# An encoder block's feed-forward: the change of halves, the border between its two products and its last steps rearranged

## The chip, the core and the metric

The kernel runs on one core of a Trainium2 chip. The metric is the device time of one execution in microseconds (us). The engines are PE (TensorE, matrix products), DVE (VectorE), ACT (ScalarE), POOL (GpSimd) and SP (SyncE, which here issues every transfer of this part from one queue). Each engine takes its instructions in a fixed order: one that waits holds up all that stand behind it on that engine, and the same holds for the transfers that SP issues.

## What is computed

One layer of a hybrid encoder (a recurrent and an attention group side by side, then a feed-forward), S = 2048 tokens, D = 1024 columns, 4096 hidden units. The change touches only the second sub-layer and the closing norm:

```
h2 = rms_norm(x, norm2_g) * (1 + scale2) + shift2
ff = square(relu(h2 @ w_ff1)) @ w_ff2
x = x + gate2 * ff
return rms_norm(x, final_g)
```

## The kernel before

The feed-forward (from some 1360 us to the end) is two matrix products in single precision. Each product takes seven products of block sums instead of eight products of blocks (Strassen's scheme); `LEFT` and `RIGHT` name for each of the seven, m = 1 to 7, the blocks whose sum or difference is its left and right operand. Every operand is split into a coarse half `hi` and a rest `lo` (`halves`: ACT rounds, DVE or POOL subtracts), and hi·hi, hi·lo and lo·hi are added up in PSUM. A sum or difference of blocks is made by `signed` (L1218), on the engine that its caller names.

**First product (FF1).** The tokens are two halves, a = 0 and 1. The hidden units are 16 block pairs p. `steps1` lists 224 steps (a, m, p), in the order of m 2, 4, 5, 3, 1, 6, 7 for one p after the other. A step is 12 matmuls of 128x512. `w1_prep` makes a step's left operand from two loaded blocks of W1, three steps ahead: `signed` on POOL where m takes two blocks, `hi` on ACT, `lo` on DVE (L1222, L1223), into one of six slots. The right operands (the normed tokens, `bks`) stand in SBUF for a whole half: `build2` writes those of m = 2, 4, 5, 3 by transposes, `b_prep` makes those of m = 1, 6, 7 in four chunks each: two loads from DRAM (`st<-Dh`, L1290, L1293), `signed` on POOL, `halves`. `sums2` makes the block sums of the second half ahead and stores them (`Dhc`); near the end of the first half `b_prep(1, m)` loads these and writes all seven operands anew. `evac1` adds the seven products to the four output blocks of p, applies relu and square, makes the sums which the second product needs as its right operands, and `put` (L1330) stores them to `Dhx[m][p]`.

**Second product (FF2).** `ORD2` = 4, 2, 7, 3, 5, 1, 6 is the order of m, `steps2` goes over 16 p for each m: 112 steps of 24 matmuls (8 token tiles by 3). `ld2` (L1488, L1491) loads two blocks of W2 and the hidden operand, three steps ahead; `prep2`, two steps ahead, makes the sum on DVE, `halves` it into `wf`, rounds the hidden operand on ACT (L1508) and takes its rest on POOL (L1510). At the last p of each m the tiles are finished one after the other, three matmuls apart, and `evac2` adds each to `C`, the output in SBUF. The gate is multiplied later: `resid` (L1545 times `gate2`, L1549 plus x1 loaded into `xt`), except that m = 6 gets it in `prep2` (L1500). `final` is the closing norm of a tile of 128 tokens by 1024: ACT squares and sums (L1555), the reciprocal root goes over DVE and one POOL instruction (`rstd_g`, L299 to L306), DVE scales (L1559), SP stores 512 KB (L1560). `finals` runs `resid` and `final` during m = 6; the second half of the tiles gets its `final` when its last product is done.

All first loads of FF2 stand in the program behind the last `put` of FF1. A list scheduler decides the order of the instructions of an engine near that of the program; the rows under "The change" show it.

Of the kernel before, what the change touches and what calls it, by code (L numbers as in the profile page):

```python
# [17 lines left out]
P = 128  # L18
S = 2048
# [37 lines left out]
def block_kernel(ctx: ExitStack, tc, x, vecs, pos, w_ada, b_ada, fg, w_in, lwa, lwx, w_out, w1, w2, cst, out):  # L57
# [412 lines left out]
    xrn = [sbt("L8", (P, S + 8)) for j in range(4)]  # L470
# [792 lines left out]

    def w1_prep(s):
# [14 lines left out]
    def b_prep(a, m):  # L1279
# [5 lines left out]
        def load(k):  # L1285
            t = [sbt("st", (P, 512))]
            if a and sg:
                SY.dma_start(t[0], Dhc[m][:, k])
            else:
                SY.dma_start(t[0], Dh2[a][x_ // 10, x_ % 10][:, k])  # L1290
                if sg:
                    t.append(sbt("st", (P, 512)))
                    SY.dma_start(t[1], Dh2[a][y_ // 10, y_ % 10][:, k])  # L1293
            q.append(t)
# [117 lines left out]

    PB = ("mm", "g", "tr", "mm", "g", "tr", "mm", "g")
# [4 lines left out]
    xslot += [t[:, 512 * e:512 * (e + 1)] for t in (sbt("bc", (P, D)), sbt("bc", (P, D))) for e in range(2)]  # L1418
# [4 lines left out]
    loads = [(p, u) for p in list(range(2, NP)) + list(range(NP)) for u in (1, 0)]  # L1423
# [3 lines left out]
    for s, (a, m, p) in enumerate(steps1):  # L1427
        if s == 6:
# [12 lines left out]
        w, (hi, lo) = wslot[(s + 4) % 6], bks[m]  # L1441
# [30 lines left out]
    BUFS.update({"C": NT, "xr": 4, "w2": 4, "wf": 4, "xt": 2, "row": 2})  # L1472
    sb[0] = ctx.enter_context(tc.tile_pool(name="f2", bufs=1, reuse_waits="tile"))
    ORD2 = (4, 2, 7, 3, 5, 1, 6)
    steps2 = [(m, p) for m in ORD2 for p in range(NP)]
    N2 = len(steps2)
    C = {}
    gate2, fgb = sbt("row", (P, D)), sbt("row", (P, D))
    raws2, wts2, hraw, hids = {}, {}, {}, {}
    TILES = {i: [8 + 4 * (i - 1) + e for e in range(4)] + [4 * (i - 1) + e for e in range(4)] for i in (1, 2)}  # L1480

    def ld2(s):
        m, p = steps2[s]
        x_, sg, y_ = RIGHT[m]
        t = sbt("w2", (P, 2, 512))
        for i, blk in enumerate((x_, y_) if sg else (x_,)):
            r0, j = (p + NP * (blk // 10 - 1)) * P, blk % 10 - 1
            SY.dma_start(t[:, i], w2[r0:r0 + P, 512 * j:512 * (j + 1)])  # L1488
        raws2[s] = (t[:, 0], t[:, 1])
        hraw[s] = sbt("xr", (P, 2, 512))  # L1490
        SY.dma_start(hraw[s], Dhx[m][p])  # L1491

    def prep2(s):
        m, p = steps2[s]
        x_, y_ = raws2.pop(s)
        if RIGHT[m][1]:
            t = sbt("st", (P, 512))
            signed(V, t, x_, RIGHT[m][1], y_)
            if m == 6:
                V.tensor_tensor(t, t, gate2[:, 512:], ALU.mult)  # L1500
        else:
            t = x_
        w = sbt("wf", (P, 2, 512), F32R)
        halves(t, w[:, 0], w[:, 1], V)
        wts2[s] = w
        r_ = hraw.pop(s)
        h = sbt("L8", (P, 2, 2, 512), F32R)
        A.activation(h[:, 0], r_, AF.Copy)  # L1508
        for e in range(2):
            G.tensor_tensor(h[:, 1, e], r_[:, e], f(h[:, 0, e]), ALU.subtract)  # L1510
        hids[s] = h.rearrange("p s a t -> p s (a t)")
# [136 lines left out]
```

## Time and profile before

| | |
|---|---|
| three runs | 2720.13, 2720.20, 2723.26 us; median 2720.2 us |
| the profiled execution | 2720.57 us, of which the span of the trace is 2718.7 us |
| busy share of the span | PE 94 %, DVE 61 %, ACT 40 %, POOL 44 % |
| mean granted clock of PE | 0.949 |
| HBM read and written | 330 MB and 153 MB, 178 GB/s over the span |

PE is busy nearly all the time. In the profile's forty slices the PE digit falls to 7 or 8 near 1400 us and at some later places, and to 6 in the last slice. The average shares of the other engines say little here: each of these stretches has a bound of its own, which the rows further down show.

### The profile page before, as it was taken

How to read it: one execution, taken by the hardware profiler on the slowest of the kernel's cores; microseconds unless marked ns; L12 is line 12 of the kernel's file. 1: busy time of each engine (PE TensorE's matmuls, PEld its weight loads, DVE VectorE, ACT ScalarE, POOL GpSimd, SP SyncE). 2: the span in 40 equal slices, each digit the busy share in tenths (PEclk: the TensorE clock that was granted, in tenths of full speed). 3: DMA queues.
4: the chain of work that ended last, by engine and by line, in shares of the span. 5: the costliest groups of instructions: out<-in, count | busy, mean ns of one | idle time of the engine just before them, and what ended most of it. 6: DMA issues, size and time to landing. Idle time of an engine off the chain costs nothing.

```text
span 2718.7 us, 32852 instructions
## 1 busy us (share of the span) xinstructions
PE 2542.2 (94%) x11321; PEld 2075.0 (76%) x11321; DVE 1656.9 (61%) x2963; ACT 1093.5 (40%) x1701; POOL 1200.8 (44%) x914
## 2 busy tenths in 40 slices
PE   4998988999999999999879999899998999999996
PEld 3776767778888888887757877688886888888885
DVE  6588777974444444436767657977774224312688
ACT  2243675571122222222455445655553323232223
POOL 2343444642012211131357667766556445544544
PEclk9998989998898888899989999999998999999998
DMA  6765356566544455547766666644437465536554
GB/s 266 266 225 186 96 178 211 203 163 159 122 109 118 117 132 140 125 141 235 243 202 214 204 195 209 209 152 155 140 129 276 164 209 187 170 121 210 191 201 176
DMA packets 267491, 486.01 MB, mean 179 GB/s; under 512 B 88874, under 2 KB 122406, under 8 KB 259754
## 3 DMA queue, kind: packets, MB, share of 16 engines
q1 hardware_dynamic: 267324, 483.92, 55.4%
q8 instruction: 89, 1.46, 0.2%
q14 instruction: 78, 0.64, 0.1%
HBM read 330.45 MB, written 153.19 MB: 178 GB/s over the span
## 4 chain that ended last, share of the span: by engine, by line
PE 36%; POOL 6%; DVE 5%; DMA 5%; issue 3%; ACT 1%; SPq 0%; POOLq 0%; DVEq 0%; ACTq 0%
PE pmm L89 15%; PE pg L89 13%; PE ptr L89 8%; POOL st L1218 3%; DMA st<-Dh 3%; POOL ry L301 1%; DVE L L1223 1%; POOL t L1380 1%; DMA Dhc<-st 1%; POOL L L1510 0%; DVE C L1545 0%; DVE C L1549 0%; DVE L L1200 0%; POOL L L1381 0%; DMA r<-in_w 0%
## 5 line engine op out<-in xcount | busy, mean ns | idle before, releaser
L1510 POOL TENSOR_TENSOR L<-xr,L 128x512 fp32r<-128x512 f32 x224 | 317.5, 1438 | 285.9 <-ACT L L1508 278.7
L89 PE MATMUL pmm<-hT,wh 128*128 128x512 f32 x1536 | 376.1, 401 | 5.9 <-POOL hT L341 3.3
L89 PEld LDWEIGHTS pmm<-hT,wh 128*128 128x128 f32 x1536 | 293.6, 193 | 78.3 <-POOL hT L341 7.7
L89 PE MATMUL pmm<-wf,L 128*128 128x512 f32 x1008 | 292.4, 398 | 17.8 <-ACT L L1508 12.8
L89 PE MATMUL pg<-wf,L 128*128 128x512 f32 x1008 | 290.0, 396 | 0.0
L858 DVE CUSTOM_DVE_ANT_0 junk<-ptr,mb 128x256 bf16<-128x256 f32 (+2 forms) x384 | 140.1, 365 | 174.3 <-PE ptr L89 157.3
L89 PEld LDWEIGHTS pmm<-wf,L 128*128 128x128 f32 x1008 | 190.5, 189 | 65.2 <-ACT L L1508 13.2
L912 ACT ACTIVATE t<-pmm 128x512 f32<-128x512 f32 x160 | 94.8, 596 | 353.5 <-PE pmm L89 352.3
L1223 DVE TENSOR_TENSOR L<-st,L 128x512 fp32r<-128x512 f32 x167 | 191.4, 1151 | 63.3 <-ACT L L1222 62.0
L89 PEld LDWEIGHTS pg<-wf,L 128*128 128x128 f32 x1008 | 190.7, 189 | 45.2
L257 POOL TENSOR_TENSOR wh<-r,wh 128x512 fp32r<-128x512 f32 x88 | 139.8, 1610 | 173.5 <-DVE wh L95 106.1
L301 POOL TENSOR_TENSOR ry<-rv,mhalf 128x1 f32<-128x1 f32 x80 | 51.5, 645 | 350.4 <-DVE rv L299 341.3
L89 PE MATMUL ptr<-wf,L 128*128 128x512 f32 x672 | 193.9, 397 | 0.0
L1218 POOL TENSOR_TENSOR st<-r,r 128x512 f32<-128x512 f32 x96 | 135.9, 1423 | 109.3 <-DVE L L1223 94.7
L89 PE MATMUL pmm<-hT,hT 66*128 66x256 f32 (+5 forms) x672 | 177.1, 399 | 0.0
L1223 DVE TENSOR_TENSOR wf<-st,wf 128x512 fp32r<-128x512 f32 x80 | 59.8, 747 | 190.6 <-ACT wf L1222 190.6
L1222 ACT ACTIVATE L<-st 128x512 fp32r<-128x512 f32 x168 | 105.5, 628 | 163.6 <-POOL st L1218 84.9
L89 PE MATMUL ptr<-hT,hT 128*128 128x256 f32 (+5 forms) x672 | 163.6, 390 | 4.1 <-DVE mc L858 4.0
L1222 ACT ACTIVATE wf<-st 128x512 fp32r<-128x512 f32 x80 | 50.4, 631 | 281.7 <-PE pg L89 216.5
L89 PE MATMUL pg<-t,L 128*66 128x192 f32 (+2 forms) x756 | 159.0, 348 | 1.8 <-POOL L L1051 1.8
L89 PE MATMUL pmm<-hT,L 128*128 128x512 f32 x576 | 149.7, 408 | 10.0 <-ACT L L1222 7.1
L89 PEld LDWEIGHTS pmm<-hT,hT 128*128 128x128 f32 (+1 forms) x672 | 148.8, 278 | 9.1 <-issue 2.6
(326 smaller groups left out, 5276.3 us busy)
## 6 DMA issues: line engine op xcount, KB each, us to landing
xr<-Dhx SPq DMA_DIRECT2D x112, 512.0 KB
w<-in_w SPq DMA_DIRECT2D x192, 256.0 KB
r<-in_w SPq DMA_DIRECT2D x64, 512.0 KB
Dhx<-t SPq DMA_DIRECT2D x128, 256.0 KB
L<-in_w_ada SPq DMA_DIRECT2D x24, 1024.0 KB
r<-in_w_in SPq DMA_DIRECT2D x40, 512.0 KB
st<-Dh SPq DMA_DIRECT2D x72, 256.0 KB
r<-in_x SPq DMA_DIRECT2D x26, 512.0 KB
```

What stands on the lines that cost most here:

```text
L89: T.matmul(o, l, r, start=st, stop=sp, skip_group_check=True)
L257: G.tensor_tensor(w[:, 1, cs], raw[:, cs], f(w[:, 0, cs]), ALU.subtract)
L301: G.tensor_tensor(y, v_, mhalf[:, 0:1], ALU.pow)
L858: V.tensor_tensor_reduce(junk[:, 0:nk], p_[:, e, 0:nk], mb1[:, off:off + nk], 1.0, -3e38, ALU.add, ALU.max, mc[:, idx:idx + 1])
L912: A.activation(pf, pS, AF.Exp)
L1218: eng.tensor_tensor(o, a, b, ALU.add if sign > 0 else ALU.subtract)
L1222: A.activation(hi, raw, AF.Copy)
L1223: lo_eng.tensor_tensor(lo, raw, f(hi), ALU.subtract)
L1380: G.tensor_tensor(x6, x6, h, ALU.subtract)
L1510: G.tensor_tensor(h[:, 1, e], r_[:, e], f(h[:, 0, e]), ALU.subtract)
```

## The change

1. Half change: the second half takes the block pairs in the order 15, 0, 1, ..., 14. The seven W1 operands of p = 15 stay in their slots from the end of the first half (there are seven slots then, the seventh in a `bc` buffer) and are neither loaded nor made again. `w_slot` deals the slots out in turn.
2. `signed` of W1 goes to DVE for all of the first twelve steps, and after that for m = 1, 5 and 6; m = 2 and 7 stay on POOL.
3. `b_prep(0, m)` loads its chunks into the four halves of two `bc` buffers (`braw`) instead of into `st` buffers.
4. The first two steps of FF2 are loaded (into `r4` buffers) and made ready (weights in W1 slots, hidden operands in `hT` buffers, half a gate row in `st`) during the last steps of FF1, and multiplied straight behind its last step. The other loads of FF2 stand behind that, and the full gate row (L1581 of the changed kernel) ahead of them.
5. The gate goes into W2 in `prep2` (one multiplication per step, 128x1024 for m = 1, 6 and 7, 128x512 for the rest). `C` is preset with x1 by 16 transfers of 512 KB, two in each of eight steps, so `evac2` only adds or subtracts, all on DVE. `resid` and its loads go.
6. `ff2_mm`: the last two p of each m (the last four for m = 6) are multiplied tile by tile, so a tile's sum is complete every 6 matmuls (every 12 for m = 6) instead of every 3.
7. The last norm: the tiles of TILES[1] get `final` during m = 6. For TILES[2], `halfway` takes the squares of the first 512 columns and multiplies them by the norm's weights during m = 1; `final2` does what is left after a tile's last product. Stores of TILES[2] are 256 KB.
8. `xrn`, a buffer of an earlier stage, is 56 columns wider.

The core of the diff:

```diff
-    xrn = [sbt("L8", (P, S + 8)) for j in range(4)]
+    xrn = [sbt("L8", (P, S + 64))[:, 0:S + 8] for j in range(4)]
...
-    steps1 += [(a, m, p) for a in range(2) for p in range(0 if a else 2, NP) for m in OA + OB]
+    steps1 += [(0, m, p) for p in range(2, NP) for m in OA + OB]
+    steps1 += [(1, m, p) for p in [NP - 1] + list(range(NP - 1)) for m in OA + OB]
...
     def w1_prep(s):
-        _, m, p = steps1[s]
+        a, m, p = steps1[s]
+        if a and p == NP - 1:
+            wuse[s] = wts1[m]
+            return
...
-            signed(G, t, x_, sg, y_)
-        w = wslot[(s + 4) % 6]
+            signed(V if s < 12 or m in (1, 5, 6) else G, t, x_, sg, y_)
+        w = wuse[s] = wts1[m] = w_slot()
...
         def load(k):
-            t = [sbt("st", (P, 512))]
-            if a and sg:
-                SY.dma_start(t[0], Dhc[m][:, k])
+            if a:
+                t = [sbt("st", (P, 512))]
+                SY.dma_start(t[0], Dhc[m][:, k] if sg else Dh2[a][x_ // 10, x_ % 10][:, k])
             else:
+                t = [braw[2 * (k % 2) + e] for e in range(2)]
                 SY.dma_start(t[0], Dh2[a][x_ // 10, x_ % 10][:, k])
...
+        t = sbt("w2" if s > 1 else "r4", (P, 2, 512))
...
+        hraw[s] = sbt("xr" if s > 1 else "r4", (P, 2, 512))
...
+        if sg and x_ % 10 != y_ % 10:
+            V.tensor_tensor(raw.rearrange("p a c -> p (a c)"), raw.rearrange("p a c -> p (a c)"), gate2[0],
+                            ALU.mult)
+        if sg:
+            t = sbt("st", (P, 512))
+            signed(V, t, raw[:, 0], sg, raw[:, 1])
+        if not sg or x_ % 10 == y_ % 10:
+            V.tensor_tensor(t, t, g_, ALU.mult)
+        w = sbt("wf", (P, 2, 512), F32R) if s > 1 else w_slot()
...
+        if s == N1 - 3:
+            gate2.append(sbt("st", (P, 512)))
+            SY.dma_start(gate2[0], Dbc[1][:, 0:512])
+            ld2(0)
+            ld2(1)
...
+        if s >= N1 - 2:
+            prep2(s - N1 + 2)
...
+    def ff2_mm(s, group, evac=None):
...
+        pend.append(s)
+        if NP - group <= p < NP - 1:
+            return
+        for i in range(8):
+            ts = slice(i * P, (i + 1) * P)
+            for q in pend:
...
+    for s in range(2):
+        ff2_mm(s, 2)
     stage.close()
...
+            signed(V, C[t][:, d], C[t][:, d], sg, pt)
+        if m == 6:
+            side.append(final2(i))
+            step(3)
+
+    fgb, gate2[0] = sbt("row", (P, D)), sbt("row", (P, D))
+    SY.dma_start(gate2[0], Dbc[1])
...
+    def halfway(i):
+
+        xt = C[TILES[2][i]][:, 0:512]
+        A.activation(junk[:, 0:512], xt, AF.Square, accum_out=ssa[:, i:i + 1])
+        yield
+        G.tensor_tensor(xt, xt, fgb[:, 0:512], ALU.mult)
+
+    def final2(i):
...
+        A.activation(junk[:, 512:], xt[:, 512:], AF.Square, accum_out=ss)
+        yield
+        V.tensor_tensor(ss, ss, ssa[:, i:i + 1], ALU.add)
+        for r in rstd_g(ss, D):
+            yield
+        A.activation(xt[:, 0:512], xt[:, 0:512], AF.Copy, scale=r[:, 0:1])
+        SY.dma_start(out[t * P:(t + 1) * P, 0:512], xt[:, 0:512])
+        V.scalar_tensor_tensor(xt[:, 512:], xt[:, 512:], r[:, 0:1], fgb[:, 512:], ALU.mult, ALU.mult)
+        SY.dma_start(out[t * P:(t + 1) * P, 512:], xt[:, 512:])
...
+        if s > 2:
+            for t in x1q[:2]:
+                SY.dma_start(C[t], Dx1[t])
+            del x1q[:2]
```

**Order on POOL, at the start of FF1.** Before, while the second half's last transposes are built (`r_...` are blocks of W1, `st<-st` are the chunks of `b_prep`):

```order
314 L1218 TENSOR_TENSOR st_10723<-st_10723,st_10725 128x512
315 L1218 TENSOR_TENSOR st_10751<-st_10751,st_10753 128x512
316 L1218 TENSOR_TENSOR st_10769<-r_1636_10660 128x512
317 L1218 TENSOR_TENSOR st_10755<-st_10755,st_10757 128x512
318 L1218 TENSOR_TENSOR st_10818<-r_1621_10595,r_1609_10514 128x512
319 L1218 TENSOR_TENSOR st_10762<-st_10762,st_10764 128x512
320 L1218 TENSOR_TENSOR st_10791<-st_10791,st_10793 128x512
321 L1218 TENSOR_TENSOR st_10908<-r_1609_10514,r_1621_10595 128x512
322 L1218 TENSOR_TENSOR st_10928<-st_10928,st_10930 128x512
323 L1218 TENSOR_TENSOR st_10946<-r_1621_10595,r_1609_10514 128x512
```

And in the changed kernel, at the same place:

```order
311 L1218 TENSOR_TENSOR bc_10647<-bc_10647 128x512
312 L1218 TENSOR_TENSOR bc_10646<-bc_10646 128x512
313 L1218 TENSOR_TENSOR bc_10647<-bc_10647 128x512
314 L1218 TENSOR_TENSOR bc_10646<-bc_10646 128x512
315 L1218 TENSOR_TENSOR bc_10647<-bc_10647 128x512
316 L1218 TENSOR_TENSOR bc_10646<-bc_10646 128x512
317 L1218 TENSOR_TENSOR bc_10647<-bc_10647 128x512
318 L1218 TENSOR_TENSOR bc_10646<-bc_10646 128x512
319 L1218 TENSOR_TENSOR st_10998<-r_1636_10660,r_1635_10658 128x512
```

The sums of W1 that stood between the chunks have left POOL, the chunks stand together, and they use two `bc` buffers in turn.

**Order on SP, at the border of FF1 and FF2.** Before (`Dhx<-` are the last stores of FF1, `w<-in_w` and `xr<-Dhx` the operands of the first steps of FF2):

```order
993 L1330 DMA Dhx_161<-bc_10646 128x512
994 L1488 DMA w_2320_16000<-in_w 128x512 x2
995 L1491 DMA xr_16003<-Dhx_164 128x1024
996 L1488 DMA w_2322_16005<-in_w 128x512 x2
997 L1491 DMA xr_16008<-Dhx_164 128x1024
998 L1488 DMA w_2324_16010<-in_w 128x512 x2
999 L1491 DMA xr_16013<-Dhx_164 128x1024
1000 L1573 DMA row_15998<-Dbc_89 128x1024
```

And in the changed kernel (the loads of steps 0 and 1 stand some 15 rows earlier):

```order
996 L1337 DMA Dhx_161<-bc_10647 128x512
997 L1581 DMA row_16050<-Dbc_89 128x1024
998 L1436 DMA w_2323_16053<-in_w 128x512 x2
999 L1439 DMA xr_16056<-Dhx_164 128x1024
1000 L1436 DMA w_2325_16058<-in_w 128x512 x2
1001 L1439 DMA xr_16061<-Dhx_164 128x1024
```

The gate row has moved ahead of the loads of step 2 and later. In the built program its buffer lies where the hidden operand of step 1 lies (`hT`), and the transfer waits for the last matmul of step 1.

## Rows read from the trace of the kernel before

**Rows 1.** Windows table: stretch, us, busy PE PEld DVE ACT POOL, clock, DMA share, GB/s.

```profile
1380.00:1420.00 40.00, 26.43 (x101) 18.38 (x99) 23.26 (x24) 20.66 (x34) 20.87 (x15) 0.76 0.55 182
1740.00:1780.00 40.00, 32.98 (x130) 25.10 (x131) 37.09 (x37) 22.14 (x40) 35.74 (x23) 0.96 0.49 168
1980.00:2020.00 40.00, 40.00 (x173) 32.22 (x172) 30.01 (x35) 22.89 (x39) 24.64 (x17) 1.00 0.35 124
2060.00:2100.00 40.00, 35.17 (x140) 27.88 (x141) 20.59 (x20) 16.26 (x20) 29.64 (x20) 0.87 0.94 352
2620.00:2660.00 40.00, 39.28 (x169) 31.40 (x167) 38.91 (x55) 10.35 (x15) 18.20 (x12) 1.00 0.68 232
2700.00:2719.00 19.00, 0.80 (x4) 0.32 (x2) 14.24 (x47) 5.97 (x12) 5.83 (x7) 0.63 0.55 221
```

**Rows 2.** Timeline of PE, start of FF1: start, us, what [idle before <-releaser].

```profile
1379.20 2.96 PE L89 MATMUL ptr<-hT,L 128*128 128x512 f32 x12
1381.99 0.60 PE L322 MATMUL ptr<-ck,L 128*128 128x128 f32 x4
1387.37 1.22 PE L89 MATMUL pmm<-wh,L 128*128 128x512 f32 x2 [4.78 <-ACT L L1222]
...
1436.25 2.98 PE L89 MATMUL pmm<-hT,L 128*128 128x512 f32 x12
```

**Rows 3.** Timeline of POOL in the same stretch.

```profile
1408.26 1.27 POOL L1218 TENSOR_TENSOR st<-st,st 128x512 f32<-128x512 f32 x1 [7.66 <-DMA st<-Dh]
```

**Rows 4.** Timeline of PE, 1575 to 1650 us.

```profile
1578.87 0.63 PE L89 MATMUL pg<-wh,L 128*128 128x512 f32 x2
...
1647.89 2.49 PE L89 MATMUL pmm<-wh,L 128*128 128x512 f32 x10
```

**Rows 5.** Timeline of PE, 1715 to 1765 us, the change of halves.

```profile
1717.79 3.19 PE L89 MATMUL pg<-L,L 128*128 128x512 f32 x12
1723.64 0.73 PE L89 MATMUL pmm<-hT,L 128*128 128x512 f32 x2 [2.66 <-ACT L L1222]
...
1761.06 2.96 PE L89 MATMUL pmm<-hT,L 128*128 128x512 f32 x12
```

**Rows 6.** Groups by line and form, 1780 to 2040 us: busy, mean ns | idle before.

```profile
L1223 DVE TENSOR_TENSOR L<-st,L 128x512 fp32r<-128x512 f32 x67 | 77.2, 1154 | 4.3 <-ACT L L1222 4.3
...
L1218 POOL TENSOR_TENSOR st<-r,r 128x512 f32<-128x512 f32 x38 | 49.2, 1295 | 91.0 <-DVE L L1223 91.0
...
L1223 DVE TENSOR_TENSOR L<-r,L 128x512 fp32r<-128x512 f32 x26 | 17.9, 689 | 0.0
```

**Rows 7.** Timeline of all engines, border of FF1 and FF2.

```profile
2049.01 2.92 PE L89 MATMUL pg<-L,L 128*128 128x512 f32 x12
...
2057.50 0.86 SPq L1488 DMA_DIRECT2D w<-in_w  x2
...
2062.18 0.69 DVE L1218 TENSOR_TENSOR st<-w 128x512 f32<-128x512 f32 x1 [7.48 <-DMA w<-in_w]
...
2064.70 2.15 PE L89 MATMUL pmm<-wf,L 128*128 128x512 f32 x3 [12.76 <-ACT L L1508]
...
2069.21 1.25 PE L89 MATMUL pmm<-wf,L 128*128 128x512 f32 x3
```

**Rows 8.** Groups by line and form, 2080 to 2590 us.

```profile
L1500 DVE TENSOR_TENSOR st<-st,row 128x512 f32<-128x512 f32 x7 | 11.7, 1671 | 0.2
```

**Rows 9.** Timelines of PE and of all engines, the last 60 us.

```profile
2660.39 0.73 PE L89 MATMUL pmm<-wf,L 128*128 128x512 f32 x2 [1.11 <-DVE wf L1223]
...
2695.92 0.69 DVE L1535 TENSOR_TENSOR C<-pmm,C 128x512 f32<-128x512 f32 x1 [3.02 <-PE pmm L89]
...
2696.70 1.06 ACT L1555 ACTIVATE junk<-C 128x1024 bf16<-128x1024 f32 x1 [7.75 <-DVE C L1535]
...
2698.15 0.55 POOL L301 TENSOR_TENSOR ry<-rv,mhalf 128x1 f32<-128x1 f32 x1 [7.94 <-DVE rv L299]
```

**Rows 10.** The chain of waits, its last long piece: start, us, what.

```profile
2713.84 1.28 DVE C L1559
```

More of the change, by code (lines that the diff above doesn't have):

```diff
@@ L1410, in block_kernel, with ld2, prep2 @@
         run(b)
+    ORD2 = (4, 2, 7, 3, 5, 1, 6)
+    steps2 = [(m, p) for m in ORD2 for p in range(NP)]
+    N2 = len(steps2)
+    C = {}
+    raws2, wts2, hraw, hids, loaded, prepped = {}, {}, {}, {}, set(), set()
+    TILES = {i: [8 + 4 * (i - 1) + e for e in range(4)] + [4 * (i - 1) + e for e in range(4)] for i in (1, 2)}
+    gate2 = []
+    def ld2(s):
+        loaded.add(s)
+        m, p = steps2[s]
+        x_, sg, y_ = RIGHT[m]
+        t = sbt("w2" if s > 1 else "r4", (P, 2, 512))
+        for i, blk in enumerate((x_, y_) if sg else (x_,)):
+            r0, j = (p + NP * (blk // 10 - 1)) * P, blk % 10 - 1
+            SY.dma_start(t[:, i], w2[r0:r0 + P, 512 * j:512 * (j + 1)])
+        raws2[s] = t
+        hraw[s] = sbt("xr" if s > 1 else "r4", (P, 2, 512))
+        SY.dma_start(hraw[s], Dhx[m][p])
+    def prep2(s):
+        prepped.add(s)
+        m, p = steps2[s]
+        x_, sg, y_ = RIGHT[m]
+        raw = raws2.pop(s)
+        g_ = gate2[0][:, 512 * (x_ % 10 - 1):512 * (x_ % 10)]
+        t = raw[:, 0]
+        if sg and x_ % 10 != y_ % 10:
[7 more added lines that the diff above has]
+        w = sbt("wf", (P, 2, 512), F32R) if s > 1 else w_slot()
+        halves(t, w[:, 0], w[:, 1], V)
+        wts2[s] = w
+        r_ = hraw.pop(s)
+        h = sbt("L8" if s > 1 else "hT", (P, 2, 2, 512), F32R)
+        A.activation(h[:, 0], r_, AF.Copy)
+        for e in range(2):
+            G.tensor_tensor(h[:, 1, e], r_[:, e], f(h[:, 0, e]), ALU.subtract)
+        hids[s] = h.rearrange("p s a t -> p s (a t)")
     PB = ("mm", "g", "tr", "mm", "g", "tr", "mm", "g")
@@ L1422, in block_kernel @@
     w1_load(1, 0)
-    loads = [(p, u) for p in list(range(2, NP)) + list(range(NP)) for u in (1, 0)]
+    loads = [(p, u) for p in list(range(2, NP)) + list(range(NP - 1)) for u in (1, 0)]
     after, prev = [], None
@@ L1468, in block_kernel @@
+    pts = []
+    for s in range(2):
+        ff2_mm(s, 2)
     stage.close()
[L1472 removed]
+    BUFS.update({"C": NT, "row": 2, "xr": 4, "w2": 4, "wf": 4})
     sb[0] = ctx.enter_context(tc.tile_pool(name="f2", bufs=1, reuse_waits="tile"))
[L1474 to L1479, printed above, removed]
@@ L1493, in prep2 @@
[L1493 to L1511, printed above, removed]
+    for t in range(NT):
+        C[t] = sbt("C", (P, D))
@@ new lines, in block_kernel @@
+    fin = early()
+    for s in range(2, N2):
+        m, p = steps2[s]
+        for q in range(s, min(s + 4, N2)):
+            if q not in loaded:
+                ld2(q)
+        if s == 4:
+            bcast_row(fgb, fg, D)
+        if s > 2:
+            for t in x1q[:2]:
+                SY.dma_start(C[t], Dx1[t])
+            del x1q[:2]
+        for q in range(s, min(s + (4 if m == 6 and p >= 8 else 3), N2)):
+            if q not in prepped:
+                prep2(q)
+        ff2_mm(s, 4 if m == 6 else 2, evac2)
+        if m == 1 and p >= 1:
+            run(fin, 1)
+        if m == 6:
+            run(fin, 5)
```

121 lines of the change are left out of this document (37 added, 84 removed).

## The prediction

> **What bounds the kernel now.** I read the windows first, in stretches of 40 us, for the busy time of PE and the granted clock; then PE's timeline around each stretch that falls short; then the engine that PE's idle time names; last the groups by line for the price of each operation. In the steady part of the first product (FF1) PE is busy for 40.00 of 40 us at full clock [rows 1]. There a step of 12 matmuls takes 2.80 us (1379.20 to 1381.99, [rows 2]), and one of the second product (FF2), with 24, takes 5.60. Nothing done to another engine can gain time in such a stretch. The time that the feed-forward loses against this pace lies in six places:
>
> - A, start of FF1: from 1381.99 to 1436.25 eight steps are done [rows 2]; 54.3 us, less 8 x 2.80 = 22.4 and less 32 transposes (0.60 us for four, so at most 4.8) leaves 27.1 us. The first row with idle time names ACT at L1222, but ACT waits for POOL's sum, and POOL has waited 7.66 us for a chunk from DRAM [rows 3]. POOL takes the sums of W1 and those of the chunks in one order, so a W1 sum whose data are long there stands behind a transfer.
> - B, 1579 to 1648: 21 steps in 69.0 us instead of 58.8 [rows 4], 10.2 us lost. It is the same queue on POOL, now with the loads of `sums2` in it.
> - C, change of halves: 9 steps in 43.3 us instead of 25.2 [rows 5], 18.1 us lost. DVE is busy for 37.09 of 40 us and POOL for 35.74 [rows 1]: these two are full.
> - D, FF1 to FF2: the last step of FF1 begins at 2049.01 and is done 2.80 later, at 2051.81; at 2069.21 nine matmuls of FF2 (2.1 us) are done [rows 7]. 17.4 - 2.1 = 15.3 us lost: 12.9 until the first matmul, and 2.4 after it while PE runs slowly (9 matmuls in 4.5 us; the clock in this window is 0.87, [rows 1], so part of it is at the lower of the levels 1.2 and 2.4 GHz).
> - E, inside FF2: from 2064.70 [rows 7] to the last matmul's end at 2700.80 (0.80 us of PE in the last window, [rows 1]) are 636.1 us for 112 x 5.60 = 627.2; 8.9, less the 2.4 counted in D, is 6.5. DVE is busy for 38.91 of 40 us then [rows 1], and PE waits for the low halves that DVE makes late [rows 9].
> - F, tail: 2700.80 to 2718.7, 17.9 us, in which DVE alone works for 14.24 [rows 1].
>
> That makes 95 us; the change touches each of the six places.
>
> **Part by part.**
>
> *A.* The W1 sums of the first twelve steps go from POOL to DVE, so none waits behind a chunk. What is late next is the chunks themselves: twelve, in two buffers taken in turn. A chunk needs its transfer, POOL's 1.3 [rows 6], ACT's rounding and DVE's subtraction at 0.7 to 1.2 [rows 6]. One pair of chunks took POOL from one start to the next about as long as its wait of 7.66 and its sum of 1.27 together [rows 3], 8.9 us. In the new order of SP the loads of the first chunks stand ahead of the last stores of the first half's transposes; I take 1350 for the first pair (a choice: the operands of A's first steps are being made there), and six pairs then end at 1403. The third operand is wanted from step 10 on, at 1382 + 4.8 + 4 x 2.80 = 1398, and its last chunks also stand behind stores of the transposes in SP's queue. So some 5 to 8 us stay: gain 20. Ends: 25 if the chunks are never late, 8 if they come as late as now.
>
> *B.* Of five W1 sums in seven steps two stay on POOL behind `sums2`'s loads. They can stall PE less often but still do. Gain 6, between 0 and 10.
>
> *C.* Seven preparations fall away: 7 x 1.154 = 8.1 us of DVE and 5 x 1.295 = 6.5 us of POOL [rows 6]; on the other side six or seven W1 sums of the steps around come to DVE, 0.69 to 1.30 each (the price of a subtraction undisturbed on DVE and of a sum on POOL, [rows 6]), 4.5 to 8.5 us. The preparations that fall away lie just where DVE is full; half of the sums that come do too. Net 4 to 6 us of DVE and, beyond it, less waiting between the two full engines: gain 9, between 3 and 15.
> The row behind this choice: the subtraction on DVE takes 1154 ns when its source is a sum buffer and 689 ns when it is a loaded block [rows 6], the same work on the same shape, so 0.46 us of the first is not work. The Trainium skill (SBUF — State Buffer, "Who interferes with whom") says that a DVE instruction with two inputs in SBUF and a GpSimd instruction that reads SBUF exclude each other for the whole of an instruction. The trace agrees in that DVE's time is longer where POOL works. By that rule a sum moved costs DVE 0.69 and spares it a wait for 1.3 us of POOL, C would gain some 3 us more, and the sum below would be 58 instead of 55.
>
> *D.* Steps 0 and 1 of FF2 follow FF1 without a wait: 48 matmuls, 11.2 us. But the gate row stands ahead of the loads of step 2 in SP's queue and waits for the last matmul of step 1, whose operand its buffer covers. So the loads of steps 2 to 5 begin 11.2 us later than PE could use them: the stall is moved behind step 1. Its length: 0.4 for the row's issue, 1.5 for its 0.5 MB at the 352 GB/s of [rows 1], 4.7 from the first load's issue to DVE's first sum (2057.50 to 2062.18), 2.5 from there to the first matmul (2064.70) [rows 7], and the gate's multiplication, 0.7: 9.8 us. The slow start behind it costs 2.4 as now. 12.2 instead of 15.3: gain 3, between 0.5 and 5 with the multiplication at 0.7 to 1.7 and the row's transfer wholly beside the next or before it.
>
> *Gate and x1 in FF2.* One multiplication of 128x512 costs DVE 0.7 to 1.7 us (1671 ns in [rows 8], beside POOL), one of 128x1024 twice that at most. A step with the larger one has a sum, the product and a subtraction: at most 0.8 + 3.3 + 0.8 = 4.9 of 5.60 us, hidden; each us above 5.60 would be paid 48 times. The presets are two transfers of 512 KB in each of eight steps: with the step's own 1 MB that is 2.1 MB in 5.6 us, 375 GB/s, against 352 at 0.94 busy [rows 1]. Over eight steps the queue falls behind by 3 us at most, and loads run three steps (16.8 us) ahead: nothing. With the tiles finished every 6 matmuls (1.4 us), two additions of 0.69 [rows 9] just fit: nothing.
>
> *E.* The late multiplications and additions of `resid` go, 64 instructions of 128x512 at 0.69 or more, 44 us of DVE in the stretch where it is full. What comes, one product of 128x512 or 128x1024 in a step, leaves DVE under 5 of 5.60. Gain 6, between 2 and 6.5.
>
> *F.* The tiles come every 2.8 us instead of 0.7 and less is left for each, so no pile forms: from the last addition to POOL's instruction 2.2 us now with a square over 1024 columns ([rows 9], 2695.92 to 2698.15), 1.8 with 512; POOL 0.55; four small instructions of 0.2; a scaling of 512 columns, half of 1.28 [rows 10]; and 3.6 from the end of the last scaling (2715.12) to the end [rows 10]. That is 7.4, with the small gaps between them 7.5, instead of 17.9: gain 10.4, between 8 and 11.
>
> *Nothing:* the wider buffer, since it moves addresses only; and the two loads saved at the change of halves, since DMA is at 0.49 there [rows 1].
>
> **Sum.** 20 + 6 + 9 + 3 + 6 + 10.4 = 54.4 us. The profiled execution took 2720.6, so 2666.2; the median of the runs is 0.4 lower, so I say 2665.8.
>
> **Rivals.**
> 1. *The chunks and the `sums2` loads set the pace of A to C, whoever makes the W1 sums.* For it: every long wait of POOL there ends with a transfer [rows 3], and `st` buffers are still shared between these loads and the sums. Against: W1 sums on DVE need no chunk. A 8, B 0, C 3, the rest as above: 30.4 gained, 2690.
> 2. *A to C are cured, and D is shorter than I say.* For it: DVE and POOL both have less to do at the change of halves. Against: the order on SP. A 25, B 10, C 15, D 5, E and F as above: 71.4 gained, 2649. With the whole wait of D gone, which the wait on the gate row speaks against, 2640.
> 3. *Slower: DVE becomes the bound of the steady part of FF1.* DVE is busy for 30.01 of 40 us there [rows 1], 14.7 in the 19.6 us of seven steps. Three more sums at 0.69 to 1.30 make 16.8 to 18.6. If sums and subtractions stretch as the product in [rows 8] does (1.67), seven subtractions add 7 x 0.5: 22.2, 2.6 over in each of 28 periods, 73 us: 2739. It decides from 19.6 on, and turns the sign from about 21.5 on. Against it: POOL loses the same three sums, so there is less to stretch them.
> 4. *The change does not do what it says:* nothing is overlapped at the border and the slots are not free in time; 2715 to 2720.
>
> **How the numbers follow.** The forecast (2655 to 2680) 0.56, rival 1 0.22, rival 2 0.16, rival 3 0.04, rival 4 0.02. What a measurement of this kernel can tell from no change is about 0.2 %, 5.4 us. Faster by more: 0.94; within: 0.02; slower by more: 0.04. The range reaches from rival 2 without the cured border (2649, less 3 for the rule in C and in A) to rival 1 with E at its lower end (2694): 2646 to 2694.
>
> **What would show it.** In the changed profile: PE busy nearly without a gap from 1382 to 1395 and a remaining wait for the chunks of the third operand (A); fewer than 10 us lost at the change of halves (C); 11.2 us of matmuls straight after FF1, then an idle stretch of 8 to 11 us ended by ACT's rounding of the hidden operand, with the gate row's transfer issued at its start (D); no wait of PE for DVE in m = 6 (E); the end some 7.5 us after the last matmul (F). Wrong it would be if PE lost time in the steady part of FF1 or at the borders between the products of FF2, where I have put nothing.

## The result, and the profile after

The changed kernel takes 2706.1 us (median of six runs, 2701.0 to 2708.1) against 2721.2 for the kernel before: ratio 0.9939, interval 0.9927 to 0.9952. It is faster by 0.6 %, as forecast in sign; the forecast of 2665.8 and its range of 2646 to 2694 are missed. The profiled execution took 2707.8 us, its span is 2706.0.

From the windows table of the changed kernel (columns as in [rows 1]):

```profile
1540.00:1580.00 40.00, 34.82 (x141) 26.98 (x141) 24.90 (x34) 18.49 (x33) 18.58 (x14) 0.96 0.58 190
...
1740.00:1780.00 40.00, 35.99 (x148) 28.36 (x147) 36.45 (x41) 24.05 (x45) 23.00 (x15) 0.96 0.61 203
...
1860.00:1900.00 40.00, 40.00 (x178) 33.13 (x177) 34.04 (x43) 21.79 (x39) 15.37 (x10) 1.00 0.41 145
...
2220.00:2260.00 40.00, 37.34 (x153) 28.83 (x152) 39.79 (x38) 14.84 (x28) 28.54 (x19) 0.96 0.60 208
...
2620.00:2660.00 40.00, 35.15 (x146) 27.88 (x145) 33.63 (x29) 9.71 (x12) 24.61 (x14) 0.96 0.45 165
```

Two things stand out. In a full stretch PE now does 178 matmuls in 40.00 us where it did 173 [rows 1]: each has become shorter. And there are stretches that fall short where none did before: 1540 to 1580, and 2220 to 2260 with DVE at 39.79.

The shorter matmul is seen plainly between the starts of whole steps in PE's timeline. Before, in the second half of the first product, 2.80 us for twelve:

```profile
1800.17 2.96 PE L89 MATMUL pmm<-hT,L 128*128 128x512 f32 x12
1802.97 2.96 PE L89 MATMUL pg<-wh,L 128*128 128x512 f32 x12
```

After, 2.72:

```profile
1792.57 2.88 PE L89 MATMUL pmm<-hT,L 128*128 128x512 f32 x12
1795.29 2.88 PE L89 MATMUL pg<-L,L 128*128 128x512 f32 x12
```

So each place can be compared at the kernel's own pace. The table sums, for each stretch of steps, the time between the starts of its matmuls less 2.796 (before) or 2.72 us (after) for each twelve; the tail is counted from the end of the last matmul to the end of the span. A holds the transposes too (3 to 5 us in each of these kernels). "FF" is the time from the first matmul of FF1 to the end. The columns e2 to e15 are kernels of the experiments below.

| us lost | before | after | pad alone (e2) | sums late (e4) | e9 | e15 |
|---|---|---|---|---|---|---|
| pace, twelve matmuls | 2.796 | 2.72 | 2.72 | 2.72 | 2.72 | 2.72 |
| A, steps 0 to 19 | 33.0 | 21.2 | 33.5 | 21.9 | 21.9 | 19.2 |
| B, steps 20 to 104 | 10.3 | 32.5 | 15.0 | 20.8 | 18.7 | 18.8 |
| C, steps 105 to 125 | 18.1 | 12.1 | 21.0 | 10.1 | 10.4 | 9.4 |
| D, border of FF1 and FF2 | 15.6 | 16.9 | 15.1 | 18.3 | 17.9 | 12.5 |
| borders m = 2 to 7, 5 to 1 | 0 | 11.2 | 0 | 11.4 | 10.3 | 14.4 |
| E, m = 6 | 8.0 | 7.4 | 9.9 | 7.6 | 1.3 | 1.3 |
| F, tail | 18.0 | 13.2 | 18.1 | 13.0 | 13.3 | 9.9 |
| FF | 1354.5 | 1335.5 | 1331.1 | 1324.4 | 1314.7 | 1306.7 |

FF is 19.0 us shorter. The span is only 12.7 shorter, since FF1 starts later in this execution (1370.46 against 1364.17); in the profiled executions of all kernels here that start lies between 1363.6 and 1374.8. It varies without an edit that could move it: e9 and e16, which are alike up to there, have 1371.5 and 1365.3. Whether the wider buffer has a share in it is not shown.

**B.** The longest waits of the changed kernel from 1500 to 1650 us (engine, line, waited for: us in total, times, longest):

```profile
POOL st L1218 <- DMA st<-Dh: 44.9, 11, 7.6
...
DVE st L1218 <- POOL st L1218: 30.6, 7, 5.3
```

One of them in the timeline:

```profile
1517.73 1.28 POOL L1218 TENSOR_TENSOR st<-st,st 128x512 f32<-128x512 f32 x1 [3.69 <-DMA st<-Dh]
...
1519.04 0.69 DVE L1218 TENSOR_TENSOR st<-r 128x512 f32<-128x512 f32 x1 [4.45 <-POOL st L1218]
...
1520.85 0.68 DVE L1223 TENSOR_TENSOR L<-st,L 128x512 fp32r<-128x512 f32 x1
...
1521.59 2.01 PE L89 MATMUL pmm<-hT,L 128*128 128x512 f32 x5 [3.10 <-DVE L L1223]
```

One can see what happens: the sum of W1 has left POOL's queue, but it writes an `st` buffer which a block sum of `sums2` on POOL still holds, and that sum waits for DRAM. Now DVE stands for 4.45 us, and behind it a low half that was ready to be made and that PE waits for.

**D.** Timeline of all engines at the border of the two products:

```profile
2051.45 0.96 PE L89 MATMUL pmm<-L,hT 128*128 128x512 f32 x3 [0.49 <-DVE t L1359]
...
2057.29 0.97 PE L89 MATMUL pg<-L,hT 128*128 128x512 f32 x3 [1.58 <-DVE t L1382]
...
2062.86 0.84 PE L89 MATMUL pg<-L,hT 128*128 128x512 f32 x3
2063.74 0.32 SPq L1581 DMA_DIRECT2D row<-Dbc  x1
2064.11 0.90 SPq L1436 DMA_DIRECT2D w<-in_w  x2
...
2069.58 0.69 DVE L1218 TENSOR_TENSOR st<-w 128x512 f32<-128x512 f32 x1 [10.29 <-DMA w<-in_w]
...
2072.66 2.14 PE L89 MATMUL pmm<-wf,L 128*128 128x512 f32 x3 [8.96 <-ACT L L1462]
```

The gate row is issued when the last matmul of step 1 is done, and PE then stands for 8.96 us: the stall of [rows 7] moved behind step 1, as forecast (9.8). What I had not seen is the first step of FF2 waiting for PSUM banks that the last additions of FF1 have yet to read (the first two rows): that step loses 4.6 us. In e3 (below), with all W1 sums on POOL, it loses nothing, so this too comes from the work that the change gave to DVE.

**Borders in FF2.** DVE's and PE's timeline where m = 2 ends and m = 7 begins:

```profile
2226.73 2.31 DVE L1450 TENSOR_TENSOR w<-w,row 128x1024 f32<-128x1024 f32 x1
...
2230.93 1.67 DVE L1218 TENSOR_TENSOR st<-w 128x512 f32<-128x512 f32 x1
2232.52 1.78 DVE L1223 TENSOR_TENSOR wf<-st,wf 128x512 fp32r<-128x512 f32 x1
...
2239.67 1.28 DVE L1218 TENSOR_TENSOR C<-C,pmm 128x512 f32<-128x512 f32 x2
...
2241.10 0.93 PE L89 MATMUL pmm<-wf,L 128*128 128x512 f32 x3 [1.91 <-DVE C L1218]
```

The first tile's sum is complete before 2229.7, but DVE comes to the two additions at 2239.67, and PE waits for the bank.

**Tail.** DVE, ACT and POOL for the last two tiles; the last matmul starts at 2692.6:

```profile
2697.63 0.75 DVE L1614 SCALAR_TENSOR_TENSOR C<-C,ry,row 128x512 f32<-128x512 f32 x1
2698.30 0.68 DVE L1218 TENSOR_TENSOR C<-C,pg 128x512 f32<-128x512 f32 x1
...
2699.07 0.63 ACT L1607 ACTIVATE junk<-C 128x512 bf16<-128x512 f32 x1 [0.72 <-DVE C L1218]
...
2700.26 0.55 POOL L301 TENSOR_TENSOR ry<-rv,mhalf 128x1 f32<-128x1 f32 x1 [3.43 <-DVE rv L299]
```

The chain that I added up for one tile is right: 2698.30 to 2706.0 are 7.7 us, forecast 7.5. But the addition of the last tile, due at 2692.9, stands on DVE behind the scaling of the tile before it, and that behind ACT and POOL: the tiles follow each other by 3 to 4 us, PE gives one every 2.72.

### The profile page after: what moved, and what is told of

Read it like the earlier page. It is cut to its first block, busy times and chain, and to the rows that moved or that the text cites. A ratio compares the mean times of both kernels' runs of the same rounds, so it can differ in the third digit from the quotient of the medians.

```text
span 2706.0 us, 32891 instructions
## 1 busy us (share of the span) xinstructions
PE 2524.4 (93%) x11321; PEld 2074.4 (77%) x11321; DVE 1849.0 (68%) x3116; ACT 1073.5 (40%) x1694; POOL 1083.7 (40%) x821
## 4 chain that ended last, share of the span: by engine, by line
PE 22%; DVE 14%; DMA 8%; issue 6%; ACT 3%; POOL 3%; SPq 1%; DVEq 0%; POOLq 0%; ACTq 0%
PE pmm L89 9%; PE pg L89 7%; PE ptr L89 5%; DMA w<-in_w 3%; DVE L L1223 2%; DMA st<-Dh 2%; DVE wf L1223 1%; DVE C L1218 1%; ACT t L1333 1%; DVE w L1450 1%; POOL st L1218 1%; DVE w L1456 1%; DMA bc<-Dh 1%; DVE st L1218 1%; ACT t L1334 1%
## 5 line engine op out<-in xcount | busy, mean ns | idle before, releaser
L1464 POOL TENSOR_TENSOR L<-xr,L 128x512 fp32r<-128x512 f32 x220 | 337.5, 1557 | 237.8 <-ACT L L1462 237.7
L89 PE MATMUL pmm<-wf,L 128*128 128x512 f32 x990 | 278.1, 393 | 18.1 <-ACT L L1462 9.0
L89 PE MATMUL pg<-wf,L 128*128 128x512 f32 x990 | 276.1, 392 | 1.0 <-DVE C L1218 1.0
L1333 ACT ACTIVATE t<-t 128x512 f32<-128x512 f32 x128 | 80.9, 632 | 289.5 <-DVE t L1353 103.0
L89 PE MATMUL ptr<-wf,L 128*128 128x512 f32 x660 | 184.7, 393 | 0.6 <-DVE C L1218 0.5
L89 PE MATMUL pmm<-hT,L 128*128 128x512 f32 x576 | 145.9, 402 | 10.3 <-DVE L L1223 9.3
L89 PEld LDWEIGHTS ptr<-hT,hT 128*128 128x128 f32 (+1 forms) x672 | 142.3, 278 | 13.7 <-DVE mc L858 6.8
L89 PE MATMUL pg<-hT,L 128*128 128x512 f32 x576 | 141.9, 394 | 6.0 <-DVE L L1223 5.2
L89 PEld LDWEIGHTS ptr<-wf,L 128*128 128x128 f32 x660 | 124.8, 190 | 28.2 <-DVE C L1218 2.3
```

The lines of the kernel that those rows point to most:

```text
L89: T.matmul(o, l, r, start=st, stop=sp, skip_group_check=True)
L1333: A.activation(t, t, AF.Relu)
```

## The experiments

The kernels e1, e3, e4 and e10 start from the changed kernel, e2 from the kernel before, the others from e4 or one of its successors. Ratios are to the kernel before on the same chip.

### Addresses alone

e1 undoes `(P, S + 64))[:, 0:S + 8]` to `(P, S + 8))` in the changed kernel, e2 makes this edit alone in the kernel before, e10 takes `S + 16`.

> The changed kernel with the buffer of the earlier stage as narrow as before, so that only addresses go back. In the changed profile twelve matmuls of the feed-forward start 2.72 us apart in the steady stretches, before it was 2.80. Theory (the addresses of the operands set the pace of the matmuls): the pace goes back to 2.80, 5376 matmuls at 6.7 ns more make 36 us: about 2740 us, slower than the kernel before. Rival (the pace comes from another part, for instance the order or fewer reads by other engines): 2.72 stays, 2706 us.

> The kernel before with the wider buffer alone. Theory (addresses): the steady pace falls to 2.72 us for twelve matmuls and the time to about 2685 us, below the whole change at 2706, with the stalls of before at their places. Rival (pace from another part, as predicted): 2720 us, pace 2.80.

> The changed kernel with the buffer of the earlier stage 8 columns wider than before instead of 56, so that its slots lie 8256 bytes apart: at multiples of 64 bytes, but no longer all at the same place within 256 bytes. Theory (what counts is that the two operands of a matmul lie alike within 256 bytes): the pace is that without the pad, 2.79 us for twelve matmuls, about 2715 us as in e1_no_pad. Rival (a multiple of 64 bytes is enough): 2.72 us and the time of the changed kernel, 2706 us.

e1: 2715.7 us, 0.9967 (0.9953 to 0.9981). e2: 2701.3 us, 0.9911 (0.9891 to 0.9931). e10: 2718.2 us, 0.9975 (0.9963 to 0.9987). The steps of e1, e2 and e10 in PE's timeline, in this order:

```profile
1804.63 2.96 PE L89 MATMUL pg<-hT,L 128*128 128x512 f32 x12
1807.42 2.96 PE L89 MATMUL ptr<-hT,L 128*128 128x512 f32 x12
```

```profile
1803.83 2.88 PE L89 MATMUL pg<-wh,L 128*128 128x512 f32 x12
1806.55 2.88 PE L89 MATMUL pmm<-wh,L 128*128 128x512 f32 x12
```

```profile
1801.55 2.95 PE L89 MATMUL ptr<-hT,L 128*128 128x512 f32 x12
1804.34 2.96 PE L89 MATMUL pmm<-hT,L 128*128 128x512 f32 x12
```

The pace follows the pad in all three, 2.79, 2.72 and 2.79: the address theory holds, and the last section shows it inside one run as well. The times expected for e1 and e2 (2740 and 2685) were missed: the pad moves the time by less than 34 us, because stretches where another engine is late do not run faster with a faster PE. In e2, B and C lose 15.0 and 21.0 at the new pace, 10.3 and 18.1 at the old. The two runs also say what the other parts of the change are worth. At the old pace (e1) they gain 8.2 us. At the new one they cost some 8 us by the ratios of e2 and of the whole change, whose intervals overlap a little, and 4.4 us of FF in the profiles.

### The sums of W1

e3 and e4 change one line of `w1_prep`:

```diff
-            signed(V if s < 12 or m in (1, 5, 6) else G, t, x_, sg, y_)
+            signed(G, t, x_, sg, y_)                                       # e3
+            signed(V if s < 12 or a and m in (1, 5, 6) else G, t, x_, sg, y_)  # e4
```

> The changed kernel with all sums of W1 blocks on POOL, as before the change. Theory (in the stretch from 1500 to 1660 us DVE's sums wait for a buffer that a DRAM sum on POOL holds, and the low halves wait behind them): the 32 us lost there fall to the 10 of before, while the start of FF1 loses some 9 us more: about 2693 us. Rival (the loss there comes from the transfers of the DRAM sums and not from where the W1 sums are made): 2706 to 2715 us, the stalls stay.

> The changed kernel with W1 sums on DVE for the first twelve steps and in the second half of FF1 alone; in the first half, where the DRAM sums run, they stay on POOL. Theory (DVE's queue behind a buffer held by a DRAM sum): the loss from 1500 to 1660 us falls from 32 to some 10 us and the start keeps its gain: about 2684 us, 9 us faster than with all sums on POOL. Rival (transfers of the DRAM sums): 2706 us.

e3: 2690.9 us, 0.9879 (0.9859 to 0.9899). e4: 2693.8 us, 0.9881 (0.9857 to 0.9905). B falls from 32.5 to 18.1 (e3) and 20.8 us (e4): it was DVE's queue. It does not fall to the expected 10, and e4 misses its 2684; what stays is near e2's 15.0. At the start e3 loses 29.5 and e4 21.9: there the sums on DVE do gain. At the change of halves e3 loses 17.2 and e4 10.1, so the sums of the second half help there. They cost some of it again: e3 loses nothing in the steady part of FF1 and in the first step of FF2, e4 2.7 and 4.6 us. The two do not differ in time beyond their intervals. e4 is the base of what follows.

### The border of the two products

e5 takes four steps early instead of two (`s > 3` for `s > 1` in `ld2` and `prep2`, two loads and two preparations more), and puts the row, issued behind the loads of steps 4 and 5, on other buffers. e12 has the same with the row first, on e9 (below):

```diff
-    for s in range(2):
+    for s in range(4):
+        if s > 1:
+            prep2(s)
         ff2_mm(s, 2)
...
+    fgb, gate2[0] = sbt("row", (P, D)), sbt("row", (P, D))
+    SY.dma_start(gate2[0], Dbc[1])
+    ld2(4)
+    ld2(5)
```

> The kernel of e4_sums_late, with four steps of the second product loaded and prepared during the last steps of the first instead of two, the loads of steps 4 and 5 issued ahead of the gate row, and the row's buffer put where nothing late lies. Theory (the idle 9 us behind step 1 are only the row's wait for the last matmul of step 1 and the transfers behind it): the idle stretch goes, about 11 to 13 us less than e4, 2682 us. Rival (the last stores of the first product hold SP's queue, or the engines cannot prepare steps 2 and 3 in time): a stall of the same size a few steps later, 2691 to 2695 us.

> The kernel of e9_out_act with four steps of the second product prepared early as in e5_loads_early, but the gate row issued ahead of the loads of steps 4 and 5. In e5 step 4 waited for the gate row, which stood behind a load that waited. Theory: the idle stretch behind the early steps falls from about 9 us in e9 (4.6 plus waits in e5) to under 3, and the time is 3 to 7 us below e9. Rival (the additional preparations crowd DVE in the last steps of the first product, so what is saved behind the border is lost ahead of it): within 2 us of e9.

e5: 2695.5 us, 0.9891 (0.9874 to 0.9907), no gain on e4; D 19.0. PE's timeline shows its rival:

```profile
2070.13 0.80 PE L89 MATMUL pmm<-wf,L 128*128 128x512 f32 x1 [4.61 <-ACT wf L1222]
```

and DVE's that step 4 waited for the row, which came behind a load that itself waited:

```profile
2067.73 3.36 DVE L1456 TENSOR_TENSOR st<-st,row 128x512 f32<-128x512 f32 x2 [3.67 <-DMA row<-Dbc]
```

e12: 2682.3 us, 0.9853 (0.9838 to 0.9869), e9 has 0.9849: within 2 us, as its rival said. The idle stretch behind the early steps is gone and D falls from 17.9 to 11.3. Of these 11.3 us 10.6 are lost in the first step of FF2, where e9 loses 4.6: PE waits there for the last low halves and additions of FF1 on DVE, which fits the rival, that the additional preparations crowd DVE there; no run separates it. The border of m = 2 and 7 grows from 5.2 to 9.3; why is not shown.

### The borders inside the second product

e7 (on e4) multiplies no steps tile by tile except for m = 6. e8 (on e4) puts the gate's wide product on POOL for the first three steps of m = 7 and 1. e14 (on e9) leaves it out for these steps and e16 (on e9) for all steps of m = 7 and 1, so these two do not compute the block. e17 (on e15) puts a fence behind the last additions:

```diff
+        if m in (2, 5) and i == 7:
+            V.scalar_tensor_tensor(gate2[0][:, 0:1], C[t2][:, 512:513], 0.0, gate2[0][:, 0:1], ALU.mult, ALU.add)
```

> The kernel of e4_sums_late, where the last steps of a product are no longer multiplied tile by tile (m = 6 still). It loses 5.6 us each at the borders from m = 2 to 7 and from m = 5 to 1. Theory (DVE has taken up the three gate products of 1024 columns of the next steps ahead of the additions): the losses there stay or grow, since the additions only come later: 2694 to 2700 us. Rival (the tile by tile order makes the two additions of a tile the bound, 1.38 us against 1.36): the losses go, 2683 us.

> The kernel of e4_sums_late, with the gate's product of 1024 columns on POOL instead of DVE for the first three steps of m = 7 and m = 1. Theory (DVE's gate products ahead of the additions): the losses of 5.6 us at these two borders fall to 1 to 2 us each, about 2686 us. Rival (the additions alone are the bound, or POOL becomes late with the rest of the hidden operand instead): 2694 us or more.

> The kernel of e9_out_act without the gate's product of 1024 columns for the first three steps of m = 7 and of m = 1, which leaves the gate out of six of the 112 products of W2. e8_gate_pool, with these products on POOL, did not cure the borders, so it is open whether they are the cause. Theory (DVE's work ahead of the additions is too much, these products first): the 9 to 11 us lost at the two borders fall under 4. Rival (sums and low halves of the next steps alone keep the additions late): 8 us or more stay.

> The kernel of e9_out_act without the gate's product for all 32 steps of m = 7 and m = 1, so that the gate is left out of these. In e14 the places of the products that were left out were taken by those of later steps: five of them still stood on DVE ahead of the additions. Theory (DVE takes up work of later steps ahead of the additions, and the products of 1024 columns are the largest part of it): the 9 to 11 us at the two borders fall under 4. Rival (sums alone make the additions late as well): 7 us or more stay.

> The kernel of e15_stores_act with one small instruction on DVE behind the last additions of m = 2 and m = 5, which writes an element of the gate row with its own value and reads the last tile, so that the products of later steps can only come after the additions. Theory (it is DVE's order): the loss at the two borders falls from 13 us to under 4 and the time by about 9 us. Rival (DVE has too much work there in any order): the loss moves into the first steps of the next product, and the time stays within 3 us.

| | time, us | ratio (interval) | lost at the two borders, us |
|---|---|---|---|
| e7 | 2690.2 | 0.9870 (0.9856 to 0.9885) | 18.7 |
| e8 | 2698.6 | 0.9900 (0.9885 to 0.9914) | 22.9 |
| e14 | 2684.8 | 0.9864 (0.9846 to 0.9882) | 11.1 |
| e16 | 2670.3 | 0.9808 (0.9793 to 0.9822) | 0 |
| e17 | 2676.5 | 0.9826 (0.9809 to 0.9842) | 10.6 (and 1.1 just behind) |

In e7 the loss grows from e4's 11.4 us, as expected, so the tile by tile order is not what makes it; its time cannot be told from e4's. My theory had two forms. The first, that the additions come late because three products stand ahead of them, fell: with those on POOL (e8) the loss grew, left out (e14) it stayed, since DVE took up later steps. The second was that DVE's order alone is to blame. At the border of m = 2 and 7 the fence of e17 does put the additions in time, and the loss moves behind it, as the rival said; it falls from e15's 8.9 us to 6.0 there:

```profile
2222.49 0.84 DVE L1584 SCALAR_TENSOR_TENSOR row<-C,row 128x1 f32<-128x1 f32 x1
2223.37 4.52 DVE L1450 TENSOR_TENSOR w<-w,row 128x1024 f32<-128x1024 f32 x2
2227.81 3.47 DVE L1218 TENSOR_TENSOR st<-w 128x512 f32<-128x512 f32 x2
2231.21 2.31 DVE L1450 TENSOR_TENSOR w<-w,row 128x1024 f32<-128x1024 f32 x1
2233.44 3.44 DVE L1223 TENSOR_TENSOR wf<-st,wf 128x512 fp32r<-128x512 f32 x2
```

PE stands there for 3.00 us until 2235.24. At the border of m = 5 and 1 the fence does nothing. It reads a tile that m = 5 does not write, and so runs 20 us ahead of the additions:

```profile
2468.12 0.15 DVE L1584 SCALAR_TENSOR_TENSOR row<-C,row 128x1 f32<-128x1 f32 x1
...
2488.78 1.28 DVE L1218 TENSOR_TENSOR C<-C,pmm 128x512 f32<-128x512 f32 x2
```

The loss there is 5.7 us, where e15 has 5.4, so e17 tests the order at one border only. By that border and by e16, where the loss is nil at both, it is DVE's amount of work: a step's product, sum and low half take 2.3 + 1.7 + 1.8 = 5.8 us while POOL works beside them, where PE takes 5.44, and the 16 additions (8 x 1.28 = 10.2 us) come on top. Without POOL beside them the three take 1.2, 0.7 and 0.7 us, as in e17 while POOL is idle:

```profile
2236.80 0.68 DVE L1218 TENSOR_TENSOR st<-w 128x512 f32<-128x512 f32 x1
2237.40 1.21 DVE L1450 TENSOR_TENSOR w<-w,row 128x1024 f32<-128x1024 f32 x1
```

In the changed kernel they take 2.15, 1.49 and 1.48 on average from 2250 to 2290 us, 5.1 in all, and there PE is hardly held up. The additions, with one input in PSUM, keep 0.64 to 0.68 each.

### Stores and the tail

e9 (on e4) issues the eight early stores of `final` from ACT (`A.dma_start` for `SY.dma_start`). e6 (on e9) takes `final2` for two tiles at once, on vectors of two columns. e13 is e12 and e6 together. e15 is e13 with the stores of the last `build2` from ACT.

> The kernel of e4_sums_late, with the eight early stores of 512 KB issued from ACT instead of SP. In e4 SP's queue waits for a finished tile for up to 8 us in m = 6, and the loads of W2 and of the hidden operand stand behind that store. Theory (SP's queue): the loss of 7.6 us between 2600 and 2640 us falls under 2 us, 2687 us. Rival (DVE is late with its own work there): the loss stays, 2694 us; a store that waits on ACT could also hold up ACT's rounding, then more.

> The kernel of e9_out_act, with the last step of the norm taken for two tiles at a time: two squares, one chain of small instructions on two columns, two scalings. In the changed kernel a tile's addition stands on DVE behind the chain of the tile before, which goes over ACT, POOL and DVE and takes 3 to 4 us, while PE delivers a tile every 2.72. Theory (this chain between the additions sets the tail): with one chain in 5.44 us the tail from the last matmul to the end falls from 13 to 8 or 9 us, and the time by 4 to 5 us. Rival (the stores of the tail are the bound): no change.

> Both of the two edits before together on e9_out_act. They lie 600 us apart, so the gains should add: 7 to 12 us below e9 if both theories hold, 4 to 5 if only that on the tail does.

> The kernel of e13_all, with the eight stores of the last transposes issued from ACT instead of SP. At the start of the first product the chunks of the third operand stand behind these stores on SP, and POOL waits 34 us in all for chunks. Theory (the stores on SP's queue keep the chunks late): the loss between 1360 and 1440 us falls from 25 to 18 us or less and the time by about 6 us against e13. Rival (two buffers and the way over POOL, ACT and DVE set the chunks' pace): it stays within 3 us.

e9: 2683.9 us, 0.9849 (0.9834 to 0.9864), some 9 us below e4 by the ratios, whose intervals just overlap. E falls from 7.6 to 1.3. In the changed kernel SP's queue shows why:

```profile
2629.36 0.78 SPq L1436 DMA_DIRECT2D w<-in_w  x1
2637.27 0.34 SPq L1593 DMA_DIRECT2D out<-C  x1
2637.71 0.37 SPq L1439 DMA_DIRECT2D xr<-Dhx  x1
```

SP waits 7 us for one finished tile, with the loads of the next steps behind it.

e6: 2682.1 us, 0.9850 (0.9834 to 0.9866). The tail falls from 13.3 to 10.2 us in the profiles, 3 us rather than 4 to 5: a pair's chain holds two squares and two scalings, one behind the other, 0.7 us more for each of the two. In the time it cannot be told from e9. e13: 2682.0 us, 0.9845 (0.9830 to 0.9860), no better than e6 or e12 by the interval, so that the two gains add is not shown. e15: 2677.7 us, 0.9847 (0.9822 to 0.9872): A falls only from 21.6 to 19.2, which fits its rival, that the two chunk buffers set most of the pace there; no run has more buffers. Its SP queue, with no store in it, still takes the chunks two by two, some 7 us apart:

```profile
1376.25 2.12 SPq L1299 DMA_DIRECT2D bc<-Dh  x2
...
1383.33 1.16 SPq L1299 DMA_DIRECT2D bc<-Dh  x2
```

Of the kernels that compute the whole block, e17 has the lowest ratio, 0.9826 (0.9809 to 0.9842); e6, e9, e12, e13, e15 and e17 cannot be ordered among themselves, but all lie below the changed kernel at 0.9939 and the pad alone at 0.9911.

## Why the prediction was wrong, step by step

The time came out 40 us above the forecast. At the pace of each kernel, places A to F and the borders of FF2, forecast to gain 54.4 us, lost 14.0; the pace, forecast at nothing, gained 34. So two large errors point in opposite directions, and the second hides half of the first. The steps that failed, with what the runs showed:

- **"Nothing: the wider buffer, since it moves addresses only."** This step failed most in size: for the 5376 matmuls of FF1 and FF2, 448 twelves, it gains 448 x 0.076 = 34 us of PE's time at the pace of a free stretch, and 22.6 us by itself in the kernel before. The trace of before had it, in an earlier stage with matmuls of the same form, as PE's timeline shows:

```profile
299.64 6.74 PE L89 MATMUL pmm<-hT,wh 128*128 128x512 f32 x29
306.22 1.02 PE L424 MATMUL ptr<-st,ck 128*128 128x512 f32 x2
```

  29 matmuls in 6.58 us are 0.227 each, the feed-forward's were 0.233; I took the second for the matmul's price.
- **B, gain 6.** It lost 22 us, the largest error on the side that made the forecast too fast. I asked what the W1 sums would no longer wait for on POOL, not what the buffers they write wait for. Rival 1 names these shared buffers, as a reason to gain nothing; on DVE they cost more, since every low half stands behind.
- **A, gain 20:** 11.8. The mechanism (chunks are late next) is right, but they come later than I took. The forecast had the six pairs end at 1403; POOL still waits for the last chunk at 1417.77:

```profile
1417.77 1.29 POOL L1218 TENSOR_TENSOR bc<-bc 128x512 f32<-128x512 f32 x1 [1.18 <-DMA bc<-Dh]
```

- **C, gain 9:** 6.0; 12.1 us stay, where the prediction said fewer than 10, and DVE is still at 36.45 of 40 us.
- **D, gain 3:** a loss of 1.3. The row's wait was forecast and is there; left out were the banks that the first step waits for, 4.6 us.
- **"Gate and x1 in FF2: nothing."** 11.2 us lost at two borders. The bound for a step, 4.9 us, took the sum and the low half at 0.8 each; beside POOL they take 1.7 and 1.8, so a step takes up to 5.8. And a step that just fits leaves no room for 16 additions. The rule of the Trainium skill that the prediction weighed (SBUF — State Buffer, "Who interferes with whom") is borne out here: forms with two inputs in SBUF are stretched to 2.3, 1.7 and 1.8 us beside POOL, those with one input in PSUM are not. I weighed it for C, where it pointed to more gain, and not for the sum and the low half in FF2, where it spoke against the change.
- **E, gain 6:** 0.6. DVE did get free; the stores that I did not follow into SP's queue took its place.
- **F, gain 10.4:** 4.8. The chain for one tile was right, its order on DVE against the next tile's addition was not looked at.
- **Rival 3 (DVE the bound of the steady part of FF1)** did not come: DVE is at 34.04 of 40 us there and PE at 40.00. Only 2.5 us are lost near the end of it, and none in e3, with the W1 sums on POOL.

The sum is +11.8 - 22.2 + 6.0 - 1.3 - 11.2 + 0.6 + 4.8 - 2.5 = -14.0 for the places and 34 for the pace; that makes 20 us, and FF is 19.0 shorter. That the sign came out as forecast owes more to the pad, which the prediction put at nothing, than to the places that it worked out: without the pad (e1) the change gains 8.2 of the forecast 54.4 us. That is luck.

## What to carry to other kernels

Compare the price of one form of instruction between stages before taking it as fixed: a difference of 3 % in the commonest matmul (22.6 us alone) outweighed seven edits to the schedule (8.2 us without it). When work moves to another engine, follow the buffer that it writes and all that stands behind it on the new engine, and count with the durations beside the engine that runs there. A queue that carries loads should not also carry stores that wait for results.

## What was not expected of the hardware

The start-to-start time of the matmuls depends on where the operands lie. In the built program of the kernel before, the `L8` slots are 8224 bytes apart and lie at 0, 32, 64, 96, 128 and 160 within 256 bytes, all other buffers at 192: 2.80 us for twelve matmuls. With slots 8256 bytes apart (e10) it is 2.79; with 8448 bytes (33 x 256) all buffers lie at the same place within 256 bytes, and it is 2.72.

e10 shows it inside one run too. In FF2 each step has 24 matmuls; its weights lie in `wf`, at 160 within 256 bytes, its hidden operand in one of the six `L8` slots in turn. Four steps in a row, with the slot at 160, 96, 32 and 224:

```profile
2184.62 0.86 PE L89 MATMUL pmm<-wf,L 128*128 128x512 f32 x3
...
2190.08 0.85 PE L89 MATMUL pmm<-wf,L 128*128 128x512 f32 x3
...
2195.58 0.86 PE L89 MATMUL pmm<-wf,L 128*128 128x512 f32 x3
...
2201.17 0.86 PE L89 MATMUL pmm<-wf,L 128*128 128x512 f32 x3
```

The step whose two operands lie alike takes 5.46 us, the next, 64 bytes apart, 5.50, and the third, 128 bytes apart, 5.59. In the kernel before, with distances of 32 to 192 bytes, steps take 5.50 at 64 and 5.58 to 5.61 at the others; with the pad, where all lie alike, 5.44. So it is the distance of the two operands that counts and not their place: in the changed kernel all lie at 32, in e2 at 0, with the same pace. Slots a multiple of 256 bytes apart do not differ, and a distance of 128 is among the slow ones. Distances of less than 32 bytes were not tried.
